# Scan of a state-space layer: all TensorE products of eight heads of a chunk given in one run

## The chip, the core and the metric

The kernel runs on one NeuronCore of a Trainium2 chip. The metric is the device time of one execution in microseconds (us), the lower the better; the time of a kernel is the median of several executions. Engines are named as in the profile: PE (TensorE) multiplies matrices, PEld is its weight load, DVE (VectorE) and ACT (ScalarE) work element by element, POOL (GpSimd) here masks tiles, SP (SyncE) issues most DMAs, and ACT issues some too. Each engine runs its own queue strictly in order and waits at an instruction until the semaphores it needs have been raised by others.

## The reference

One layer of a hybrid backbone is computed twice with the same weights: on a context of 256 tokens and on 2048 latent tokens. Each token row is normalised, multiplied by a wide input matrix, and its columns go to a scan group (Mamba-2 in chunks of 128 tokens, forward and backward) and to a convolution group; both are gated, normalised, and multiplied by an output matrix. What matters here is the scan. For one direction, with chunks of 128 tokens, 16 heads of 64 channels in two groups of eight, and a state of 128 per channel:

```python
    cb = jnp.einsum('bclgn,bcsgn->bgcls', cc, bc)
    y_diag = jnp.einsum('bgcls,bgrcls,bcsgrp->bclgrp', cb, decay_in, xg)
    decay_to_end = jnp.exp(la_cum[..., -1:] - la_cum)
    states = jnp.einsum('bclgn,bgrcl,bclgrp->bcgrpn', bc, decay_to_end, xg)
    ...
    y_off = jnp.einsum('bclgn,bcgrpn,bgrcl->bclgrp', cc, prev, jnp.exp(la_cum))
    y = (y_diag + y_off).reshape(bsz, seqlen, SSD_HEADS, p)
```

`y_diag` are the products inside a chunk, `states` is what a chunk adds to the state, and `y_off` is the part that the state before the chunk gives. `prev` is carried from chunk to chunk.

## The kernel before

The 2304 tokens are 18 tiles of 128 (tiles 0 and 1 are the context). The program has two halves of 10 and 8 tiles. In each half, an `xbc_phase` makes the columns for the scan; then `post` makes the other column blocks, 128 channels at a time, with `gab_unit` (two matrices `gb` and `ga` for the convolution group) and `silu_unit` (`sp`). Each of these blocks is a row of TensorE products of 128x512 or 128x256 in groups of three (high and low parts of both operands, lines 461 to 463). I call these the **dense products**. When both halves are done, a last phase multiplies by the output matrix (`op`).

The forward scan is `pass_a(i)`, one generator for each tile, cut in steps by `yield`. `scan` starts a new tile every seven steps, so that two tiles are in work at once, and `interleave` spreads the steps between the dense products of `post`: tiles 0 to 8 in the first half, 9 to 17 in the second. In the second half `lat_conv` stands there too: rows of very small products (`cp`, line 718), evacuated by DVE (`cvv`, line 722). For tile i and group g (eight heads, in two half-groups hq of four) `pass_a` does:

- `load_lb`: DMAs issued by ACT bring rows of decays, repeated over the partitions, into tiles `lb` (four buffers for each direction). `mask` takes `el` from it on ACT and masks it on POOL, `decay` takes four exponentials on ACT, and `mix` on DVE adds both directions and multiplies by the chunk's `cb`. The finished `lb` is the moving operand of the products inside the chunk, and its buffer is free for the next tile's DMA only when they have read it.
- `weigh(g, d)`: DVE makes `xw`, ACT rounds it to `xwh`, and DVE makes the rest `xwl`. `xwh` and `xwl` have two buffers each: a third `weigh` needs a `state` to have read its two.
- `diag(g, hq)`: four products inside the chunk, 64x128 each, into the PSUM bank `py`; `off(g)`: the part of the state, four products of 128x128 into `po`; `state(g, d)`: three products of 128x512 into `pst`, for direction d.
- `carry`, `keep`, `close`: DVE and ACT empty `po`, `pst` and `py` and store the result.

`diag`, `off` (and `qo`, `cm`, `px`, `pb` elsewhere) work on plain float32, which the profile records as two passes for each product (four products of `py` are x8); `state` and the dense products work on float32r in one pass. Transposes (`px`, half of `pb`) are one pass.

The scan's small PSUM tiles share five banks (`ss`); the dense products have three others (`mm`).

The order of each engine's queue is not the order of the text. The language's scheduler plays the program with a timeline of its own and gives each engine what is ready first; the order in the text is a priority. `InOrder` (lines 67 to 81) overrides this: while `T.on` is true, each TensorE instruction is held behind the TensorE instruction written just before it.

Of the kernel before, what the change touches and what calls it, by code (L numbers as in the profile page):

```python
# [84 lines left out]
def backbone_kernel(ctx, tc, xa, xt_in, cols, rows, wconv, conf_b, gp_row, bg_row, state0, w_mod, w_dt, w_in, w_out,  # L85
# [3 lines left out]
    V, S, T, DMA = (InOrder(tc, e) for e in (nc.vector, nc.scalar, nc.tensor, nc.sync))  # L89
# [5 lines left out]
    def bank(tag, name):  # L95
        return psp.tile([P, 512], F32, tag=tag, name=name, bufs=3 if tag == "mm" else 5)
# [633 lines left out]
    def pass_a(i):  # L730
# [37 lines left out]
        def mix(g, hq):  # L768
            a = E[g, hq, 0]
            V.tensor_tensor(a, a, E[g, hq, 1], ADD)  # L770
            V.tensor_tensor(a, a, cb[:, g, :].unsqueeze(1).to_broadcast([P, 4, P]), MUL)
# [14 lines left out]
        def weigh(g, d):  # L786
            w = pa.tile([P, 512], F32, tag="xw", name=f"xw{i}{g}{d}", bufs=1)
            wh = pa.tile([P, 512], F32R, tag="xwh", name=f"xwh{i}{g}{d}", bufs=2)
            wl = pa.tile([P, 512], F32R, tag="xwl", name=f"xwl{i}{g}{d}", bufs=2)
            c = d * NH + g * 8  # L790
            V.tensor_tensor(b3(w), b3(xt[g]), bh(WS[:, i, c:c + 8]), MUL)
            S.copy(wh, w)
            V.tensor_tensor(wl, w, wh.bitcast(F32), SUB)
            xw[g, d] = wh, wl

        def diag(g, hq):
            if hq == 0:
                py[g] = bank("ss", f"py{i}{g}")
            for t in range(4):
                h = hq * 4 + t  # L800
                j, q = h % 2, h // 2
                T.matmul(py[g][j * HD:(j + 1) * HD, q * P:(q + 1) * P], xt[g][:, h * HD:(h + 1) * HD],  # L802
                         E[g, hq, 0][:, t, :], start=True, stop=True)

        def off(g):
            if i != 0:
                po[g] = bank("ss", f"po{i}{g}")
                for q in range(4):
                    T.matmul(po[g][:, q * P:(q + 1) * P], Sf[g][:, q * P:(q + 1) * P], bc[:, 2 + g, :],  # L809
                             start=True, stop=True)  # L810

        def state(g, d):
            pst[g, d] = bank("ss", f"pst{i}{g}{d}")
            wh, wl = xw[g, d]
            T.matmul(pst[g, d], bth[:, g, :], wh, start=True, stop=False)
            T.matmul(pst[g, d], bth[:, g, :], wl, start=False, stop=False)
            T.matmul(pst[g, d], btl[:, g, :], wh, start=False, stop=True)

        def carry(g):
            if i != 0:  # L820
                V.tensor_tensor(b3(Sf[g]), b3(Sf[g]), bh(eTf[:, i, g * 8:(g + 1) * 8]), MUL)
                w = pa.tile([P, 4, P], F32, tag="yo", name=f"yo{i}{g}", bufs=1)
                V.tensor_tensor(w, po[g].rearrange("p (q l) -> p q l", l=P), el[g], MUL)
                po[g] = w
                V.tensor_tensor(Sf[g], Sf[g], pst[g, 0], ADD)
            else:
                V.tensor_copy(Sf[g], pst[g, 0])

        def keep(g):
            sb = pa.tile([P, 512], F32, tag="sb", name=f"sb{i}{g}", bufs=1)  # L830
            S.copy(sb, pst[g, 1])
            DMA.dma_start(ST[i][:, g * 512:(g + 1) * 512], sb)
# [8 lines left out]
        def close(g):  # L841
            y = yg[g]
            V.tensor_tensor(y, y, py[g].rearrange("p (q l) -> p q l", l=P), ADD)
            if i != 0:
                V.tensor_tensor(y, y, po[g], ADD)
            DMA.dma_start(YP[i][:, g * 512:(g + 1) * 512], y.rearrange("p q l -> p (q l)"))
# [37 lines left out]
        mask(1, 1)  # L884
        skip(1)
        yield
        diag(0, 0)
        off(0)
        state(0, 0)
        weigh(1, 0)  # L890
        mix(1, 0)
        decay(1, 1)
        yield
        diag(0, 1)
        state(0, 1)
        carry(0)
        weigh(1, 1)
        mix(1, 1)
        yield
        diag(1, 0)  # L900
        off(1)
        state(1, 0)
        keep(0)
        close(0)
        yield
        diag(1, 1)
        state(1, 1)
        carry(1)
        yield
        keep(1)  # L910
# [7 lines left out]
    def scan(tiles):  # L918

        gens = [pass_a(i) for i in tiles]  # L920
        live, t = [], 0
        while gens or live:
            if gens and t % 7 == 0:
                live.append(gens.pop(0))
            for g in list(live):
                if next(g, 0) == 0:
                    live.remove(g)
            t += 1
            yield
# [627 lines left out]
```

## Time and profile before

| | us |
|---|---|
| three executions | 1851.51, 1852.80, 1853.14 |
| median | 1852.80 |
| the profiled execution | 1855.05 |
| its span, first to last instruction | 1853.3 |
| first scan (tiles 0 to 8), first to last `py` | 262.5 to about 708 |
| second scan (tiles 9 to 17) | about 918 to 1306 |

The profile is one execution on the core. Busy time is the time in which an engine has an instruction running; products overlap in TensorE, so a TensorE that is busy all the time may still have room. "Idle before" is the time an engine stood still in front of an instruction, followed by what released it. The rows on which the argument rests stand in the prediction.

### The profile page before, as it was taken

Reading aid. Unit: us, or ns where it says so; the run is one execution under the profiler, and the core shown is the slowest. Engines: PE = TensorE matmul, PEld = TensorE weight load, DVE = VectorE, ACT = ScalarE, POOL = GpSimd, SP = SyncE. Lnnn points to the kernel's source line nnn. Section 1 sums busy time; section 2 is a strip of 40 time slices with the busy share of each in tenths; the row PEclk is TensorE's granted clock in tenths of the full one; section 3 lists DMA queues with packets and bytes.
Section 4 is the critical chain, followed back from the end, with each engine's and each line's share of the span. In section 5 each row is a group of like instructions: output and inputs, shape, how many; then the busy total and the mean of one; then the engine's idle time right before and its main releaser. Section 6 shows DMA issues by size and latency. Waiting matters only on the chain.

```text
span 1853.3 us, 29884 instructions
## 1 busy us (share of the span) xinstructions
PE 1793.9 (97%) x11167; PEld 1480.5 (80%) x11167; DVE 1216.5 (66%) x1847; ACT 867.1 (47%) x1960; POOL 172.2 (9%) x281
## 2 busy tenths in 40 slices
PE   5999999999999999999999889999999999999998
PEld 2888887888888888888877667777787888888886
DVE  4597857575666762687457375868347878777763
ACT  4747424444455431744235344554245545454441
POOL 1002001011111000100002011110000101111110
PEclk9999999999999999999999889999999999999999
DMA  9656566554786654545697889694977666656632
GB/s 334 215 198 238 204 212 212 190 201 162 261 267 216 222 182 145 178 170 201 195 207 225 176 239 233 229 236 176 290 223 238 194 184 167 172 171 170 185 103 80
DMA packets 304429, 375.22 MB, mean 202 GB/s; under 512 B 84246, under 2 KB 203670, under 8 KB 304284
## 3 DMA queue, kind: packets, MB, share of 16 engines
q1 hardware_dynamic: 283548, 335.56, 58.1%
q10 hardware_dynamic: 20736, 37.76, 7.3%
q8 instruction: 88, 1.44, 0.3%
q14 instruction: 57, 0.47, 0.1%
HBM read 243.66 MB, written 129.59 MB: 201 GB/s over the span
## 4 chain that ended last, share of the span: by engine, by line
PE 87%; DMA 8%; issue 1%; ACT 1%; DVE 1%; SPq 1%; POOL 0%; ACTq 0%; POOLq 0%; DVEq 0%
PE op L81 21%; PE sp L461 6%; PE sp L462 6%; PE sp L463 6%; PE xp L462 5%; PE xp L461 5%; PE xp L463 5%; PE ga L461 3%; PE ga L463 3%; PE ga L462 3%; PE gb L461 3%; PE gb L463 3%; PE gb L462 3%; DMA lb<-lt 3%; PE py L802 2%; PE po L809 2%
## 5 line engine op out<-in xcount | busy, mean ns | idle before, releaser
L766 ACT ACTIVATE lb<-lb,WB 128x128 f32<-128x128 f32 x576 | 184.5, 391 | 162.7 <-POOL lb L758 156.6
L461 PE MATMUL sp<-hh,wh 128*128 128x512 f32 (+1 forms) x640 | 240.0, 375 | 0.0
L463 PE MATMUL sp<-hh,wl 128*128 128x512 f32 (+1 forms) x640 | 237.1, 371 | 0.0
L462 PE MATMUL sp<-hl,wh 128*128 128x512 f32 (+1 forms) x640 | 237.0, 370 | 0.0
L758 POOL TENSOR_SCALAR_AFFINE_SELECT lb<-lb 128x512 f32<-128x512 f32 x144 | 109.1, 761 | 729.9 <-ACT el L755 400.5
L463 PE MATMUL xp<-hh,wl 128*128 128x512 f32 (+1 forms) x456 | 168.0, 368 | 0.0
L462 PE MATMUL xp<-hl,wh 128*128 128x512 f32 (+1 forms) x456 | 167.8, 368 | 0.0
L461 PE MATMUL xp<-hh,wh 128*128 128x512 f32 (+1 forms) x456 | 167.0, 367 | 0.0
L558 DVE SCALAR_TENSOR_TENSOR cva<-raw,cwh,cva 128x1280 f32<-128x1280 f32 (+1 forms) x96 | 141.9, 1487 | 20.4 <-ACT cva L552 18.2
L463 PEld LDWEIGHTS sp<-hh,wl 128*128 128x128 f32 x640 | 121.3, 189 | 21.1
L461 PEld LDWEIGHTS sp<-hh,wh 128*128 128x128 f32 x640 | 121.6, 190 | 20.7 <-issue 0.2
L462 PEld LDWEIGHTS sp<-hl,wh 128*128 128x128 f32 x640 | 121.6, 190 | 20.0
L461 PE MATMUL ga<-hh,wh 128*128 128x512 f32 (+1 forms) x320 | 121.3, 379 | 6.4 <-DMA wh<-whd 5.5
L75 DVE SCALAR_TENSOR_TENSOR cg<-cg,cv 128x256 f32<-128x256 f32 x240 | 123.0, 512 | 3.3
L461 PE MATMUL gb<-hh,wh 128*128 128x512 f32 (+1 forms) x320 | 120.5, 376 | 0.0
L463 PE MATMUL ga<-hh,wl 128*128 128x512 f32 (+1 forms) x320 | 119.2, 373 | 0.5 <-DMA wl<-wld 0.5
L462 PE MATMUL ga<-hl,wh 128*128 128x512 f32 (+1 forms) x320 | 119.4, 373 | 0.0
L463 PE MATMUL gb<-hh,wl 128*128 128x512 f32 (+1 forms) x320 | 119.0, 372 | 0.0
L462 PE MATMUL gb<-hl,wh 128*128 128x512 f32 (+1 forms) x320 | 118.9, 371 | 0.0
L770 DVE TENSOR_TENSOR lb<-lb,lb 128x512 f32<-128x512 f32 x72 | 50.8, 706 | 90.0 <-ACT lb L766 71.7
L638 DVE SCALAR_TENSOR_TENSOR sth<-sth,sp 128x512 f32<-128x512 f32 (+1 forms) x80 | 50.4, 630 | 75.6 <-ACT sth L637 70.7
L755 ACT ACTIVATE el<-lb 64x256 f32<-64x256 f32 x136 | 56.3, 414 | 88.8 <-DMA lb<-lt 71.2
(273 smaller groups left out, 3832.9 us busy)
## 6 DMA issues: line engine op xcount, KB each, us to landing
lb<-lt ACTq DMA_DIRECT2D x144, 256.0 KB, 4.6
wr<-in_w_in SPq DMA_DIRECT2D x88, 256.0 KB, 4.9
whd<-wh SPq DMA_DIRECT2D x44, 512.0 KB, 3.4
wld<-wl SPq DMA_DIRECT2D x44, 512.0 KB, 5.2
wh<-whd SPq DMA_DIRECT2D x44, 512.0 KB, 5.5
wl<-wld SPq DMA_DIRECT2D x44, 512.0 KB, 5.9
xT<-xb SPq DMA_DIRECT2D x18, 512.0 KB, 4.2
yp<-yg SPq DMA_DIRECT2D x36, 256.0 KB, 4.9
```

The source lines that it names most:

```text
L75: return self._tc.keep_in_program_order(getattr(self._eng, name)(*a, **k))
L81: return lambda *a, **k: self._tc.keep_in_program_order(f(*a, **k))
L461: T.matmul(ps[:, :BN], wh[:, k, :], hh[:, k, :], start=(k == 0), stop=False)
L462: T.matmul(ps[:, :BN], wh[:, k, :], hl[:, k, :], start=False, stop=False)
L463: T.matmul(ps[:, :BN], wl[:, k, :], hh[:, k, :], start=False, stop=(k == KT - 1))
L558: V.scalar_tensor_tensor(a[:, :n], raw[:, t:t + n], cwh[:, ct * 5 + t:ct * 5 + t + 1], a[:, :n], MUL, ADD)
L638: V.scalar_tensor_tensor(th, th, 1.0, ps[:, :BN], ADD, MUL)
L755: S.activation(el[g][rs, q:q + 2, :], E[g, hq, 0][rs, j::2, :], AF.Exp)
L758: G.affine_select(E[g, hq, d], E[g, hq, d], pattern=[[0, 4], [sg, P]], compare_op=ALU.is_ge, fill=NEG, base=0, channel_multiplier=-sg)
L766: S.activation(lb[:, h, :], lb[:, h, :], AF.Exp, bias=WB[:, i, c + h:c + h + 1])
L770: V.tensor_tensor(a, a, E[g, hq, 1], ADD)
L802: T.matmul(py[g][j * HD:(j + 1) * HD, q * P:(q + 1) * P], xt[g][:, h * HD:(h + 1) * HD], E[g, hq, 0][:, t, :], start=True, stop=True)
```

## The change

A new function `burst(g)` gives TensorE, in this order and without anything between, `off(g)`, both `diag(g, hq)` and both `state(g, d)`. It takes the place of the single calls, at the point where the second half of them stood. `weigh(1, 0)` and `weigh(1, 1)`, the weighting of the second group, each stand one step later than before, and `burst(1)` stands directly behind the step that has `weigh(1, 1)`.

```diff
+        def burst(g):
+            T.on = True
+            off(g)
+            diag(g, 0)
+            diag(g, 1)
+            state(g, 0)
+            state(g, 1)
+            T.on = False
+
...
-        diag(0, 0)
-        off(0)
-        state(0, 0)
-        weigh(1, 0)
         mix(1, 0)
         decay(1, 1)
         yield
-        diag(0, 1)
-        state(0, 1)
+        burst(0)
         carry(0)
-        weigh(1, 1)
+        weigh(1, 0)
         mix(1, 1)
         yield
-        diag(1, 0)
-        off(1)
-        state(1, 0)
         keep(0)
         close(0)
-        yield
-        diag(1, 1)
-        state(1, 1)
+        weigh(1, 1)
+        yield
+        burst(1)
         carry(1)
         yield
```

No instruction is added or removed. What the scheduler makes of it is shown at three places of the second half. First TensorE in tile 12, around the first group of heads. A row is the line, the operation, output<-inputs and size, and a count where rows are equal. Before, the two stretches were:

```order
L462 MATMUL ga1_5_3_10179<-hl3_7103,wh3232_1_9646 128x512
L463 MATMUL ga1_5_3_10179<-hh3_7102,wl3232_1_9645 128x512
L802 MATMUL py120_10233<-lb12000_9971,xt120_10068 64x128 x4
L809 MATMUL po120_10238<-bc12_9855,Sf0_259 128x128 x4
L815 MATMUL pst1200_10243<-xwh1200_10134,bth12_10062 128x512
L816 MATMUL pst1200_10243<-xwl1200_10135,bth12_10062 128x512
L817 MATMUL pst1200_10243<-xwh1200_10134,btl12_10063 128x512
L461 MATMUL ga1_5_3_10179<-hh3_7102,wh3232_1_9646 128x512
```

and, 18 dense products further on,

```order
L462 MATMUL gb1_5_4_10268<-hl4_7313,wh4256_1_9642 128x512
L463 MATMUL gb1_5_4_10268<-hh4_7312,wl4256_1_9641 128x512
L802 MATMUL py120_10233<-lb12010_10036,xt120_10068 64x128 x4
L815 MATMUL pst1201_10294<-xwh1201_10184,bth12_10062 128x512
L816 MATMUL pst1201_10294<-xwl1201_10185,bth12_10062 128x512
L817 MATMUL pst1201_10294<-xwh1201_10184,btl12_10063 128x512
L461 MATMUL gb1_5_4_10268<-hh4_7312,wh4256_1_9642 128x512
```

Now, at the place of the second stretch (line 81 is the helper that holds the order):

```order
L462 MATMUL gb1_5_4_10248<-hl4_7313,wh4256_1_9642 128x512
L463 MATMUL gb1_5_4_10248<-hh4_7312,wl4256_1_9641 128x512
L81 MATMUL po120_10270<-bc12_9849,Sf0_259 128x128 x4
L81 MATMUL py120_10275<-lb12000_9957,xt120_10068 64x128 x4
L81 MATMUL py120_10275<-lb12010_10036,xt120_10068 64x128 x4
L81 MATMUL pst1200_10284<-xwh1200_10134,bth12_10062 128x512
L81 MATMUL pst1200_10284<-xwl1200_10135,bth12_10062 128x512
L81 MATMUL pst1200_10284<-xwh1200_10134,btl12_10063 128x512
L81 MATMUL pst1201_10288<-xwh1201_10184,bth12_10062 128x512
L81 MATMUL pst1201_10288<-xwl1201_10185,bth12_10062 128x512
L81 MATMUL pst1201_10288<-xwh1201_10184,btl12_10063 128x512
L461 MATMUL gb1_5_4_10248<-hh4_7312,wh4256_1_9642 128x512
```

The dense row is interrupted once instead of twice, and the state's part comes first. Between this run and that of the second group (`po121`) stand 33 dense products: 9 of `gb1_5_4` and 24 of `ga1_5_4`.

The second place is ACT at the same point of tile 12, from the rounding `xwh1210` to the rounding `xwh1211` of the second group. `el130` and `lb130..` belong to the next tile, 13. Before:

```order
L746 DMA lb13000_10357<-lt1_116 128x512
L792 CAST xwh1210_10248<-xw1210_10247 128x512
L755 ACTIVATE el130_10314<-lb13000_10357 64x256 x2
L766 ACTIVATE lb13000_10357<-lb13000_10357,WB_257 128x128 x4
L746 DMA lb13010_10414<-lt1_116 128x512
L792 CAST xwh1211_10303<-xw1211_10302 128x512
L831 COPY sb120_10351<-pst1201_10294 128x512
```

Now:

```order
L746 DMA lb13000_10343<-lt1_116 128x512
L746 DMA lb13010_10414<-lt1_116 128x512
L792 CAST xwh1210_10297<-xw1210_10296 128x512
L840 COPY sb120_10331<-pst1201_10288 128x512
L755 ACTIVATE el130_10308<-lb13000_10343 64x256 x2
L755 ACTIVATE el130_10308<-lb13010_10414 64x256 x2
L622 ACTIVATE gth1_5_4_10322<-gb1_5_4_10248 128x512
L766 ACTIVATE lb13000_10343<-lb13000_10343,WB_257 128x128 x4
L766 ACTIVATE lb13010_10414<-lb13010_10414,WB_257 128x128 x4
L792 CAST xwh1211_10338<-xw1211_10337 128x512
```

Both DMAs of the next tile's `lb` now stand together, and the second rounding stands behind two `el`, a `gth` and both sets of exponentials, where it stood behind one `el` and one set.

The third place is TensorE in tile 11, first group, beside a row of the small products `cp2` of `lat_conv` (`cp2_0` and `cp2_1`, two `ss` banks, 64 products in turn). Before, the row followed the first stretch of the group:

```order
L802 MATMUL py110_9724<-lb11000_9313,xt110_9485 64x128 x4
L809 MATMUL po110_9729<-bc11_9260,Sf0_259 128x128 x4
L815 MATMUL pst1100_9734<-xwh1100_9605,bth11_9479 128x512
L816 MATMUL pst1100_9734<-xwl1100_9606,bth11_9479 128x512
L817 MATMUL pst1100_9734<-xwh1100_9605,btl11_9480 128x512
...
L718 MATMUL cp2_0_9761<-cx2_9345,kt2_9703 32x64
L718 MATMUL cp2_1_9762<-cx2_9345,kt2_9703 32x64
```

Now it stands ahead of the whole run, with six dense products between:

```order
L718 MATMUL cp2_1_9742<-cx2_9331,kt2_9703 32x64
L461 MATMUL ga1_4_3_9720<-hh3_7102,wh3104_1_9177 128x512
L462 MATMUL ga1_4_3_9720<-hl3_7103,wh3104_1_9177 128x512
L463 MATMUL ga1_4_3_9720<-hh3_7102,wl3104_1_9176 128x512
L461 MATMUL ga1_4_3_9720<-hh3_7102,wh3104_1_9177 128x512
L462 MATMUL ga1_4_3_9720<-hl3_7103,wh3104_1_9177 128x512
L463 MATMUL ga1_4_3_9720<-hh3_7102,wl3104_1_9176 128x512
L81 MATMUL po110_9813<-bc11_9254,Sf0_259 128x128 x4
L81 MATMUL py110_9818<-lb11000_9299,xt110_9485 64x128 x4
L81 MATMUL py110_9818<-lb11010_9390,xt110_9485 64x128 x4
```

The six `pst` products follow as in tile 12. Six dense products between a `cp` row and a run of a group stand also in tiles 9 (first group), 13 and 15 (second group), and twelve in tile 15 (first group).

## The prediction

> **What bounds the kernel now.** I began with the page's first and fourth parts, busy time and the chain that ended last.
>
> ```profile
> span 1853.3 us, 29884 instructions
> PE 1793.9 (97%) x11167; PEld 1480.5 (80%) x11167; DVE 1216.5 (66%) x1847; ACT 867.1 (47%) x1960; POOL 172.2 (9%) x281
> PE 87%; DMA 8%; issue 1%; ACT 1%; DVE 1%; SPq 1%; POOL 0%; ACTq 0%; POOLq 0%; DVEq 0%
> ```
>
> PE is busy 97% of the span and makes up 87% of the chain. So a change pays only if it shortens PE's own row, and costs only if it makes PE wait. The two scans differ, though, and the average hides it. The windows below are the first scan's part, the second scan, and the last phase; the columns are length, then busy time of PE, PEld, DVE, ACT and POOL, the granted clock, the DMA share and GB/s.
>
> ```profile
> 200.00:830.00 630.00, 629.10 (x3455) 527.24 (x3454) 409.48 (x645) 294.19 (x668) 56.41 (x95) 1.00 0.60 201
> 930.00:1310.00 380.00, 353.61 (x3707) 278.83 (x3706) 251.51 (x430) 173.20 (x428) 45.69 (x64) 0.95 0.80 213
> 1310.00:1853.00 543.00, 532.46 (x2570) 446.17 (x2569) 363.07 (x534) 248.78 (x597) 46.69 (x54) 1.00 0.62 182
> ```
>
> In the first scan PE stands still for 0.9 us of 630: time saved on PE is time saved. In the second it stands still for 26.4 us of 380, the clock is at 0.95, and the DMA engines are at 0.80: there PE is often the one that waits. For whom, the list of PE's waits says (total, times, longest):
>
> ```profile
> PE ga L461 <- DMA wh<-whd: 5.5, 1, 5.5
> PE px L778 <- issue: 5.3, 2, 4.1
> PE cp L718 <- DVE cvv L722: 4.4, 1, 4.4
> PE pst L815 <- DVE cvv L722: 3.5, 1, 3.5
> PE pst L815 <- ACT xwh L792: 1.7, 1, 1.7
> ```
>
> These are single long waits in the second scan, behind transfers and behind DVE and ACT work that itself waited.
>
> **What the change saves on PE.** Tile 6, first group, in the timeline (start, duration, line, tiles, count): two stretches, each from the last dense product before it to the first one behind it.
>
> ```profile
> 579.43 0.39 PE L463 MATMUL sp<-hh,wl 128*128 128x512 f32 x1
> 579.75 0.66 PE L802 MATMUL py<-lb,xt 128*64 128x128 f32 x8
> 580.33 1.16 PE L809 MATMUL po<-bc,Sf 128*128 128x128 f32 x8
> 581.25 0.47 PE L815 MATMUL pst<-xwh,bth 128*128 128x512 f32 x1
> 581.56 0.39 PE L816 MATMUL pst<-xwl,bth 128*128 128x512 f32 x1
> 581.79 0.40 PE L817 MATMUL pst<-xwh,btl 128*128 128x512 f32 x1
> 582.02 0.40 PE L461 MATMUL sp<-hh,wh 128*128 128x512 f32 x1
> ...
> 585.91 0.39 PE L463 MATMUL sp<-hh,wl 128*128 128x512 f32 x1
> 586.23 0.66 PE L802 MATMUL py<-lb,xt 128*64 128x128 f32 x8
> 586.81 0.50 PE L815 MATMUL pst<-xwh,bth 128*128 128x512 f32 x1
> 587.15 0.40 PE L816 MATMUL pst<-xwl,bth 128*128 128x512 f32 x1
> 587.39 0.40 PE L817 MATMUL pst<-xwh,btl 128*128 128x512 f32 x1
> 587.63 0.28 PE L461 MATMUL sp<-hh,wh 128*128 128x256 f32 x1
> ```
>
> Starts count here, since products overlap. Products of 512 columns follow each other by 0.23 us (581.56 to 581.79). Going from dense to `py` takes 0.32, from `py` to the first `pst` and on to the second 0.58 to the start and then 0.34. So a stretch pays for changing from one kind to the other, about 0.09 going in and 0.11 and more coming out. The stretches are 2.59 and 1.72 us, together **4.31**.
>
> The burst is not in the trace; I put it together. Dense to `po`: full-width float32 behind float32r, shown by `cm` in the last phase:
>
> ```profile
> 1470.51 0.62 PE L81 MATMUL op<-woh,pl 128*128 128x512 f32 x2
> 1470.97 0.38 PE L81 MATMUL cm<-v,ones 128*128 128x128 f32 x2
> 1471.11 0.71 PE L81 MATMUL op<-woh,ph 128*128 128x512 f32 x2
> ```
>
> Two dense products and the step to `cm` take 0.46, so going in costs the ordinary 0.23. Four `po` take 0.92 (580.33 to 581.25). `po` to `py` has no row: I add the 0.09 that `py` costs behind dense work, with bounds 0 and 0.19 (twice that, rounded). Eight `py`: 0.58 for four with their way out, and four more at the pace of a pass of `po`, 0.92/8 = 0.115, so 1.04; bounds 0.87 (the further four at half the price) and 1.16 (twice 0.58). Six `pst`: 0.82 for three with their way out (586.81 to 587.63) and three at 0.23, so 1.51. Sum 0.23 + 1.01 + 1.04 + 1.51 = 3.79, and 0.23 for the dense step that now lies elsewhere: 4.02. **A group saves 0.29 us**, bounds 0.07 and 0.55. There are 36 groups (tile 0 has no `po`; its two `py` stretches come to about the same), so 10.4 us in all, bounds 2.5 and 19.8: 5.2 in each scan.
>
> The Trainium skill speaks against this term: "TensorE: Matmul & The Clock Gate", section "Step-by-step: what each phase is for", says that TensorE pulls the next weight load ahead of running products, so that next weights load beside current work. By that alone a change of kind would be free and this term nothing; the rows (0.32 against 0.23) disagree, and the row decides.
>
> The first scan's 5.2 I count in full: PE had no idle time there, and DVE (409 of 630) and ACT (294) have room. Of the second's I count **half, 2.6**: where a transfer or DVE is what PE waits for, an earlier PE only waits longer. Bounds 0 and 5.2.
>
> **What it adds: a wait at the second burst.** Products that moved later meet inputs that are ready; the exception is `weigh(1, d)`. Its buffers `xwh` are free only after both `state(0, d)`, now at the end of the first burst, and ACT's queue has the next tile's `el` and exponentials ahead of `xwh` of (1, 1). Those need a DMA into `lb` buffers that `diag` of the first burst frees. So PE's first burst releases a DMA, ACT waits for it, and behind ACT stands PE's second burst, with all dense products behind that. Tile 12 in the trace (ACT, ACTq its DMA issues; then DVE, then the landing time over all `lb` transfers, least, median, most):
>
> ```profile
> 1082.48 0.33 ACTq L746 DMA_DIRECT2D lb<-lt  x1
> 1083.61 0.61 ACT L792 CAST xwh<-xw 128x512 fp32r<-128x512 f32 x1
> 1088.41 0.85 ACT L755 ACTIVATE el<-lb 64x256 f32<-64x256 f32 x2 [4.19 <-DMA lb<-lt]
> ...
> 1094.14 0.60 ACT L622 ACTIVATE gth<-gb 128x512 f32<-128x512 f32 x1
> 1095.10 1.28 ACT L766 ACTIVATE lb<-lb,WB 128x128 f32<-128x128 f32 x4 [0.35 <-POOL lb L758]
> ```
> ```profile
> 1092.97 0.68 DVE L793 TENSOR_TENSOR xwl<-xw,xwh 128x512 fp32r<-128x512 f32 x1
> ```
> ```profile
> DMA to landing us min/median/max: 3.0/4.6/7.9
> ```
>
> From the freed `lb` to a finished `xwl`: issue 0.33, landing 4.6, two `el` 1.70, `gth` 0.60, mask 0.35, two sets of exponentials 2.56, `xwh` 0.61, `xwl` 0.68, together 11.4; with the 5.9 that this transfer took (1082.48 to 1088.41) 12.7. From the same point PE has: six `pst` 1.51, 33 dense 7.6, into and through `po` and `py` 2.28, three `pst` 0.82, together 12.2. So it is even: nothing at the median landing, 0.5 at 5.9, 2.5 at 7.9. Tiles 12 and 16 have this order; 10 and 14 leave out one or both sets of exponentials, and the others have nothing of `lb` there, or, in the first scan, at least 9.8 us of dense work (18 products of 512 columns and 48 of 256, in tile 2) between the bursts. I take **1 us each for tiles 12 and 16: 2 us**; bounds 0 and 5.
>
> **And a wait for banks.** A stretch before held three of the five `ss` banks, so a pair of `cp` banks could still be waiting for DVE; a burst needs four. Where a `cp` row stands just ahead, the last bank of the burst must be one that `cvv` has emptied. Rows of PE and of DVE, in tile 11 and in tile 13:
>
> ```profile
> 1023.02 1.48 PE L718 MATMUL cp<-cx,kt 32*32 32x64 f32 x128
> 1139.41 1.48 PE L718 MATMUL cp<-cx,kt 32*32 32x64 f32 x128
> ```
> ```profile
> 1034.89 1.29 DVE L722 SCALAR_TENSOR_TENSOR cvv<-cp,cbb 128x512 f32<-128x512 f32 x2 [2.22 <-DMA kd<-in_wconv]
> ...
> 1143.20 1.28 DVE L722 SCALAR_TENSOR_TENSOR cvv<-cp,cbb 128x512 f32<-128x512 f32 x2
> ```
>
> DVE had emptied them 11.7 and 3.6 us after the row's end. PE has six dense products, `po`, `py` and three `pst` until then: 1.4 + 2.28 + 0.82 = 4.5. At 3.6 nothing waits. At 11.7 the burst of tile 11 waits 7.2; but the same lateness stopped PE before as well, at the next `cp` row (4.4) and at tile 11's last `pst` (3.5), and those two then shrink. I set old against new: **0**, bounds -4 (both old waits gone, the new one halved) and 10 (the five places named, 2 us each).
>
> The moved `px` (behind some eight dense products, where it stood directly behind `pb`) can cover part of its 5.3 us of waits; I leave that in the half above.
>
> **Sum.** -5.2 - 2.6 + 2.0 + 0 = -5.8 us. On the profiled execution (1855.05, span 1853.3) this gives 1849.2; that run lies 2.25 above the median of the three shown. On the median of 1852.8 it gives **1847.0 us**.
>
> **The rivals.**
> All of it arrives: no wait at the bursts, and the second scan keeps its 5.2, so 1852.8 - 10.4 = 1842.4. For it: PE's waits in the second scan are few long events, and between them it was full. Against: DMA at 0.80.
> The second scan gives all back: -5.2 + 2.0 gives 1849.6. For it: 26.4 us of idle there, none of PE's own doing.
> The saving isn't there, because `po` to `py` and the longer run cost what the second change of kind did: 0.07 a group, -2.5 + 2.0 gives 1852.3. This is also where the Trainium skill's rule above would lead. Against it: both ways into `py` above cost the same 0.32.
> Slower: the banks decide. If DVE is late at the five `cp` places by 2 us more than PE has room, PE waits 10 us, and an idle PE also loses clock, as the windows around tile 11's 3.5 us wait show:
>
> ```profile
> 1047.70:1051.10 3.40, 0.32 (x6) 0.08 (x2) 1.33 (x3) 2.35 (x8) 0.64 (x1) 1.00 0.01 3
> 1051.10:1054.50 3.40, 2.98 (x11) 2.59 (x12) 3.36 (x7) 2.02 (x1) 0.40 (x1) 0.50 0.29 88
> ```
>
> 3.4 us at half the clock lose 1.7 us; two such add 3.4. Together -5.8 + 10 + 3.4 = +7.6, so 1860.4. It comes out slower than before once the five waits pass 1.2 us each, a `cvv` that is done 5.7 us after its row. For it: 11.7 in one of the two rows. Against: 3.6 in the other. The Trainium skill, "TensorE: Matmul & The Clock Gate" (section "HAM oscillation — how this bites in real kernels"), sets the bound at idle gaps over about 3.4 us; by it waits of 2 us would lose no clock, and this rival would end at 1857.0.
>
> **How the numbers follow.** Forecast 0.40, all arrives 0.20, second scan gives back 0.20, no saving 0.07, slower 0.13. The range 1839.5 to 1857 takes in the first four, the lower end for a change of kind dearer than I took (a few us of the way to 0.55 a group), and the near half of the slower case (1852.8 to 1857). A measurement here tells 0.2% (3.7 us) from no change, so the limits are 1849.1 and 1856.5: faster 0.60 (most of the forecast, all of the first rival, a quarter of the second), same 0.27, slower 0.13.
>
> **What would show it.** A burst in the new timeline should take about 3.8 us from dense to dense where nothing waits, `po` first at 0.23. PE's busy time in the first scan should shrink with the span and its idle time stay near 0.9 us. In the second scan waits of `pst` for `xwl` or `xwh` should appear at tiles 12 and 16, with `lb` landings behind them on ACT, and one for a bank at tile 11, behind `cvv`. The prediction is wrong in size if a burst takes 4.2 or more, and wrong in kind if PE's idle time in the first scan grows by several us, or if the waits of the second sum to over 35 us.

## The result, and the profile after

| | before | after |
|---|---|---|
| median of 12 executions, us | 1854.9 | 1845.4 |
| ratio of the times, with its 95% interval | | 0.9946 (0.9931 to 0.9962) |
| profiled execution (span), us | 1855.05 (1853.3) | 1848.29 (1846.6) |

The change made the kernel faster by 0.54%, about 10 us: on the median of 1852.8 this is 1842.8 (1840.0 to 1845.8). Forecast were 1847.0, with 1839.5 to 1857.0. The sign and the range hold, but the time came from other places than the forecast said. One of the twelve executions before took 6255 us; it counts in the median and not in the ratio. The first and fourth parts of the page after:

```profile
span 1846.6 us, 29922 instructions
PE 1784.9 (97%) x11167; PEld 1489.9 (81%) x11167; DVE 1212.8 (66%) x1847; ACT 866.2 (47%) x1960; POOL 170.6 (9%) x281
PE 77%; DMA 10%; ACT 4%; DVE 4%; issue 3%; SPq 1%; POOL 0%; ACTq 0%; DVEq 0%; POOLq 0%
```

The 38 instructions more are none of those counted for the five engines. PE lost 9.0 us of busy time (1793.9 to 1784.9) and its share of the chain fell from 87 to 77%: more of the chain now runs through DMAs, ACT and DVE. PE's longest waits in the two scans (total, times, longest; `issue` is time in which PE waited for nothing that the profile shows):

```profile
PE sp L461 <- DVE sth L638: 7.6, 2, 4.9
PE pst L81 <- DVE cvv L722: 7.5, 2, 6.8
PE pst L81 <- ACT xwh L792: 4.9, 1, 4.9
PE cp L718 <- issue: 3.5, 2, 2.6
PE px L778 <- issue: 3.1, 2, 2.1
```

The last four are the second scan's, where 5.5 (`ga` for `wh`), 5.3 (`px`), 4.4 (`cp`) and 3.5 (`pst` for `cvv`) had led. The first is new, and in the first scan.

To see where time went I cut both runs at the same four dense products. Windows before (length, then busy time of PE, PEld, DVE, ACT, POOL, the granted clock, DMA share, GB/s), the first and the second scan:

```profile
256.79:741.45 484.66, 483.76 (x2729) 403.55 (x2728) 302.54 (x517) 217.65 (x535) 50.42 (x80) 1.00 0.62 206
925.08:1315.27 390.19, 363.80 (x3752) 287.25 (x3750) 254.69 (x435) 174.42 (x430) 45.69 (x64) 0.95 0.81 214
```

and after:

```profile
258.06:746.88 488.82, 481.15 (x2729) 409.47 (x2728) 301.64 (x517) 216.33 (x535) 50.35 (x80) 0.99 0.61 205
930.53:1308.30 377.77, 355.35 (x3751) 289.76 (x3750) 252.27 (x436) 174.93 (x430) 44.19 (x64) 0.96 0.84 221
```

Each pair holds the same products. The first scan became **4.2 us longer**: PE's idle time (length less busy) grew from 0.9 to 7.7. The second became **12.4 us shorter**: idle fell from 26.4 to 22.4, busy time by 8.5. The forecast was -5.2 and -0.6. Busy time also holds what half clock costs, which I take as half of the time that PE was busy at half clock: 0 and 15.3 us in the two scans before, 4.3 and 13.0 after. Without it **TensorE's own work fell by 6.9 us in the first scan and 6.1 in the second**.

**The saving.** The burst of tile 2's first group in the timeline (start, duration, line, tiles, count):

```profile
375.94 0.39 PE L463 MATMUL ga<-hh,wl 128*128 128x512 f32 x1
376.17 1.05 PE L81 MATMUL po<-bc,Sf 128*128 128x128 f32 x8
377.15 1.09 PE L81 MATMUL py<-lb,xt 128*64 128x128 f32 x16
378.17 0.50 PE L81 MATMUL pst<-xwh,bth 128*128 128x512 f32 x1
...
379.44 0.40 PE L81 MATMUL pst<-xwh,btl 128*128 128x512 f32 x1
379.67 0.28 PE L461 MATMUL gb<-hh,wh 128*128 128x256 f32 x1
```

It takes 379.67 - 375.94 = 3.73 us, in steps of 0.23, 0.98, 1.02 and 1.50, where 3.79 was put together. With the dense step 3.96, against 4.31 in two stretches: **0.35 a group**, 12.6 us for 36.

**The wait that wasn't foreseen.** ACT in tile 5 after: the square of an input row of the second half (`xin`), line 337, stands ahead of `sth`, which empties the dense bank:

```profile
536.21 1.06 ACT L337 ACTIVATE xin<-xin 128x1024 f32<-128x1024 f32 x1 [6.08 <-DMA xin<-in_xa]
...
537.78 0.57 ACT L840 COPY sb<-pst 128x512 f32<-128x512 f32 x1
543.28 1.06 ACT L337 ACTIVATE xin<-xin 128x1024 f32<-128x1024 f32 x1 [4.92 <-DMA xin<-in_xa]
...
544.33 0.58 ACT L637 ACTIVATE sth<-sp 128x512 f32<-128x512 f32 x1
```

and PE, which waits for that bank:

```profile
545.68 0.80 PE L461 MATMUL sp<-hh,wh 128*128 128x512 f32 x1 [4.86 <-DVE sth L638]
```

Before, the same `sth` stood between two such squares, and the second of them waited 1.5 us only:

```profile
542.22 0.57 ACT L637 ACTIVATE sth<-sp 128x512 f32<-128x512 f32 x1
544.32 1.06 ACT L337 ACTIVATE xin<-xin 128x1024 f32<-128x1024 f32 x1 [1.52 <-DMA xin<-in_xa]
```

No line of the change touches these squares, but the new order has two squares more ahead of that `sth`. SP issued the DMAs of these two at 530.43 and 537.39, the second only when the square of 536.21 had ended, so squares in a row cost a landing each. That the scheduler moved them because the products left other gaps on ACT is my reading; no run shows it.

**The two waits that were.** PE and DVE in tile 11's first burst, with the bank that `cvv` must empty:

```profile
1027.89 0.40 PE L81 MATMUL pst<-xwh,btl 128*128 128x512 f32 x1
1035.05 0.79 PE L81 MATMUL pst<-xwh,bth 128*128 128x512 f32 x1 [6.76 <-DVE cvv L722]
```
```profile
1034.30 1.29 DVE L722 SCALAR_TENSOR_TENSOR cvv<-cp,cbb 128x512 f32<-128x512 f32 x2 [11.26 <-DMA cv<-cvv]
```

7.2 was forecast here, 6.8 it is. Tile 12's second burst: ACT, then PE.

```profile
1081.20 0.40 ACT L766 ACTIVATE lb<-lb,WB 128x128 f32<-128x128 f32 x1 [3.61 <-POOL lb L758]
1081.27 0.33 ACTq L746 DMA_DIRECT2D lb<-lt  x1
...
1085.55 1.71 ACT L755 ACTIVATE el<-lb 64x256 f32<-64x256 f32 x4 [2.08 <-DMA lb<-lt]
1087.29 0.60 ACT L622 ACTIVATE gth<-gb 128x512 f32<-128x512 f32 x1
1087.90 2.44 ACT L766 ACTIVATE lb<-lb,WB 128x128 f32<-128x128 f32 x8
...
1090.25 0.60 ACT L792 CAST xwh<-xw 128x512 fp32r<-128x512 f32 x1
```
```profile
1090.90 0.79 PE L81 MATMUL pst<-xwh,bth 128*128 128x512 f32 x1 [4.89 <-ACT xwh L792]
```

This is the chain that was written down, link by link; its length is off (below).

### The profile page after: what moved, and what is told of

It reads as the page before. It is cut to its first block, busy times and chain, and to the rows that moved or that the text cites. A ratio compares the mean times of both kernels' runs of the same rounds, so it can differ in the third digit from the quotient of the medians.

```text
span 1846.6 us, 29922 instructions
## 1 busy us (share of the span) xinstructions
PE 1784.9 (97%) x11167; PEld 1489.9 (81%) x11167; DVE 1212.8 (66%) x1847; ACT 866.2 (47%) x1960; POOL 170.6 (9%) x281
## 4 chain that ended last, share of the span: by engine, by line
PE 77%; DMA 10%; ACT 4%; DVE 4%; issue 3%; SPq 1%; POOL 0%; ACTq 0%; DVEq 0%; POOLq 0%
PE op L81 21%; PE sp L461 6%; PE sp L463 5%; PE sp L462 5%; PE xp L461 4%; PE xp L462 4%; PE xp L463 4%; DMA lb<-lt 4%; PE gb L463 3%; PE gb L461 3%; PE gb L462 3%; PE ga L461 3%; PE ga L462 3%; PE ga L463 3%; PE pst L81 2%
## 5 line engine op out<-in xcount | busy, mean ns | idle before, releaser
L461 PEld LDWEIGHTS xp<-hh,wh 128*128 128x128 f32 x456 | 86.0, 189 | 14.8 <-ACT raw L546 0.5
L462 PEld LDWEIGHTS xp<-hl,wh 128*128 128x128 f32 x456 | 86.0, 189 | 14.1
```

The lines of the kernel that those rows point to most:

```text
L461: T.matmul(ps[:, :BN], wh[:, k, :], hh[:, k, :], start=(k == 0), stop=False)
L462: T.matmul(ps[:, :BN], wh[:, k, :], hl[:, k, :], start=False, stop=False)
```

## The experiments

Twelve runs, in three rounds. Ratios are to the kernel before, timed on the same chip. Diffs are against the changed kernel unless said otherwise.

| kernel | ratio (95% interval) | first scan, us | idle | second scan, us | idle |
|---|---|---|---|---|---|
| before | | 484.7 | 0.9 | 390.2 | 26.4 |
| changed | 0.9946 (0.9931 to 0.9962) | 488.8 | 7.7 | 377.8 | 22.4 |
| again | 0.9923 (0.9901 to 0.9945) | 488.5 | 7.4 | 376.1 | 24.0 |
| cvv2 | 0.9936 (0.9915 to 0.9956) | 486.6 | 6.9 | 375.9 | 22.1 |
| sq17 | 0.9932 (0.9911 to 0.9954) | 485.8 | 6.6 | 371.0 | 18.0 |
| wx13 | 0.9920 (0.9896 to 0.9943) | 487.8 | 7.2 | 372.1 | 21.2 |
| first | 0.9988 (0.9972 to 1.0005) | 486.8 | 6.9 | 385.7 | 23.3 |
| second | 0.9941 (0.9920 to 0.9963) | 484.4 | 0.4 | 382.7 | 28.4 |
| kinds | 0.9990 (0.9971 to 1.0009) | 483.5 | 5.2 | 384.7 | 30.4 |
| pyfirst | 0.9915 (0.9886 to 0.9944) | 490.0 | 8.8 | 378.3 | 26.3 |
| xlate14 | 0.9886 (0.9867 to 0.9905) | 476.6 | 0.1 | 374.5 | 22.0 |
| allfix | 0.9903 (0.9887 to 0.9919) | 480.9 | 2.3 | 375.0 | 21.4 |
| before_rows | 1.0067 (1.0044 to 1.0091) | 491.3 | 5.3 | 403.2 | 36.3 |
| after_rows | 0.9963 (0.9945 to 0.9981) | 486.7 | 7.5 | 374.4 | 20.8 |

The scans are lengths between the same dense products as above, from one profiled execution each, idle is length less PE's busy time. The profiled execution lies within 5 us of the kernel's median, except for `again` (6 above), `after_rows` (7 below), `before_rows` (11 above) and `pyfirst` (15 above), whose lengths are to be read with that. Two executions with the same order on PE, DVE, ACT and POOL differ too: the second scan took 377.8 and 376.1 us (changed, `again`).

### The three waits, one at a time

**again**: the changed kernel once more.

> The changed kernel itself, once more. Theory A (the change's own size is fixed by the order of the queues): 0.993 to 0.997 of the kernel before, a burst of 3.73 us from dense to dense where nothing waits, and the same three long waits of PE again: the last state product of tile 11's first burst behind DVE's cvv (6.8 us), the last state of tile 12's second burst behind ACT's xwh (4.9), and sp behind DVE's sth near 541 us (4.9). Theory B (the waits are accidents of one execution): at least one of the three is missing or under half as long.

Theory A holds for the waits: 6.0 us at tile 11, 5.7 at tile 12, 3.7 near 541 us. The ratio lies just below its 0.993. The waits belong to the order, not to one execution.

**cvv2**: a second buffer.

```diff
-        vt = lp.tile([P, 32, 64], F32, tag="cvv", name=f"cvv{j}", bufs=1)
+        vt = lp.tile([P, 32, 64], F32, tag="cvv", name=f"cvv{j}", bufs=2)
```

> The changed kernel with two buffers for cvv instead of one, so that DVE need not wait until the store of the row before has read the single one; the order on every engine is that of the changed kernel. Theory A (the bank wait at tile 11 is a real cost, 6.8 us of standing and some 1.5 to 2.5 us at half clock behind it): 6 to 9 us faster than the changed kernel run beside it, and the wait of pst for cvv at tile 11 is gone. Theory B (the late store is only a sign of busy DMA queues, and the row after it waits as long for another transfer): 0 to 2 us faster, with a wait of about the same length at the next cp or kd.

Theory B holds, with 0.9936 against 0.9923 for the unedited kernel beside it. The first burst of tile 11 runs through, and its second one, which had not waited, waits for `cvv` in its place. This time `cvv` is late because DVE stands 8.0 us ahead of it at a `yg`, for the DMA that stores an earlier one:

```profile
1045.34 0.77 PE L81 MATMUL pst<-xwh,bth 128*128 128x512 f32 x1 [6.31 <-DVE cvv L722]
```

**sq17**: one pair of rows swapped on ACT, by an order edge from `sth` of that block to the square of xin17.

```diff
-                    with tc.issue_after(anchor[0].ins):
+                    with tc.issue_after((anchor17 if i == 17 else anchor)[0].ins):
                         S.activation(xt, xt, AF.Square, accum_out=ms)
```

> The changed kernel with two neighbouring rows of ACT's queue swapped: the square of the input row xin17 goes behind the evacuation sth of the dense block before it, as it stood before the change. Theory A (the change cost 4.9 us there, because ACT waits for the DMA of xin17 ahead of the sth that frees the dense bank, and about 2.4 us more at half clock): 5 to 7.5 us faster than the changed kernel run beside it, no gap of PE near 541 us. Theory B (sth and PE then wait for something else in the same convoy, such as lb or the store behind SP): 0 to 3 us faster, with a wait of PE for another releaser between 540 and 575 us.

Theory B again, in its wait; the time (0.9932) is not better. The gap at 541 us is gone, and 20 us on PE waits longer than it did there (2.8 us in the changed kernel):

```profile
PE sp L461 <- DVE sth L640: 5.2, 1, 5.2
PE px L780 <- issue: 1.4, 1, 1.4
```

The square still stops ACT for 3.9 us; now other work stands behind it.

**wx13**: on ACT, `el` of tile 13's first half-group goes behind the last `xwh` of tile 12, by an order edge in `mask`.

```diff
+                    late = tc.issue_after(last_wh[0].ins) if i == 13 and (g, hq) == (0, 0) else nullcontext()
+                    with late:
-                    S.activation(el[g][rs, q:q + 2, :], E[g, hq, 0][rs, j::2, :], AF.Exp)
+                        S.activation(el[g][rs, q:q + 2, :], E[g, hq, 0][rs, j::2, :], AF.Exp)
```

> The changed kernel with the exponentials el of tile 13 (first half-group) held on ACT behind the rounding xwh of tile 12's last weighting. Theory A (tile 12's second burst waits because ACT has the next tile's el, a gth and both sets of exponentials ahead of xwh(1,1), as forecast): the wait of 4.9 us falls to about 1.5 (DVE's own xw is done 3.4 us before ACT rounded it), and the kernel is 3 to 6 us faster than the changed kernel beside it, half clock counted. Theory B (the chain through DVE, whose queue is full of cg rows there, is the later one): the wait falls by under 1 us and the time stays within 2 us.

The wait fell to what theory A says, 0.57 + 0.77 = 1.3 us, so the chain is the one described. But the gain did not come: 0.9920 against 0.9923 for the unedited kernel beside it. In tile 13's second burst, one tile later, 0.8 us of waiting for `cvv` became

```profile
1134.58 0.77 PE L81 MATMUL pst<-xwh,bth 128*128 128x512 f32 x1 [4.47 <-DVE cvv L722]
```

### Which half, and which products

**first** and **second**: the new tail of `pass_a` under `if i < 9:` or `if i >= 9:`, the old one for the other tiles.

> The run of eight heads (and the later weightings) in tiles 0 to 8 alone; tiles 9 to 17 as in the kernel before. Theory A (from the profiles: in the first scan TensorE's own work falls by 6.9 us, but ACT's queue, released in bursts, makes dense blocks wait some 7 us near 541 and 567 us, and half clock behind them costs 4): 0 to 5 us slower than the kernel before, with PE's two waits of sp for sth in the first scan and the waits of the second scan as before the change. Theory B (the forecast: the first scan keeps its saving whole): 5 to 7 us faster.

> The run of eight heads in tiles 9 to 17 alone; tiles 0 to 8 as in the kernel before. Theory A (the gain sits in the second scan: 6.0 us less work of TensorE, some 4 less waiting, 2 to 6 less at half clock): 10 to 15 us faster than the kernel before, faster than the changed kernel beside it by 0 to 5 us, and no wait of PE between 260 and 720 us beyond 1 us. Theory B (the forecast: the second scan keeps half its saving and gets new waits): 0 to 2 us faster.

`second` alone gives all of the changed kernel's gain (0.9941), as theory A says, and `first` alone gives none that is clear (0.9988; theory A, 0 to 5 us slower, was too dark). In its profile the first scan is 2.1 us longer than before and has PE's waits of 4.7 and 2.1 us at 541 and 568. The forecast's -5.2 for the first scan lies at the interval's end. But the ratio is not the first scan's alone: in `first`'s second scan PE has the order of before, while some 40 rows each of DVE and ACT stand elsewhere, and it took 385.7 us instead of 390.2. The changed kernel was not timed beside `second`; against its 0.9946 and 0.9923 of other rounds `second` is no faster.

**kinds**: the state products stand apart again.

```diff
             diag(g, 1)
-            state(g, 0)
-            state(g, 1)
...
+        state(0, 0)
+        weigh(1, 0)
         mix(1, 0)
         decay(1, 1)
         yield
         burst(0)
+        state(0, 1)
         carry(0)
-        weigh(1, 0)
+        weigh(1, 1)
         mix(1, 1)
         yield
+        state(1, 0)
         keep(0)
         close(0)
-        weigh(1, 1)
         yield
         burst(1)
+        state(1, 1)
         carry(1)
```

> The run holds only off and both diag; the state products stand apart again, state(0) a step ahead of the run and state(1) behind it, and weigh(1, d) where it stood before the change. Theory A (what costs is a change between the dense products' kind and plain float32 narrow products; a state product is a dense product in kind and costs nothing more when it stands alone): TensorE's own work in both scans within 1.5 us of the changed kernel's, pst alone between dense products at 0.23 us each, the wait of pst for xwh at tile 12 gone; the time equal to the changed kernel's or up to 5 us less. Theory B (each interruption of the dense row costs, whatever its kind): 36 more interruptions at 0.1 to 0.3 us, TensorE's own work 4 to 10 us more than in the changed kernel.

On the cost of a change of kind theory A holds. A state product between dense ones:

```profile
369.12 0.39 PE L463 MATMUL gb<-hh,wl 128*128 128x512 f32 x1
369.34 0.39 PE L815 MATMUL pst<-xwh,bth 128*128 128x512 f32 x1
369.57 0.39 PE L816 MATMUL pst<-xwl,bth 128*128 128x512 f32 x1
369.80 0.39 PE L817 MATMUL pst<-xwh,btl 128*128 128x512 f32 x1
370.02 0.39 PE L461 MATMUL gb<-hh,wh 128*128 128x512 f32 x1
```

Every step is 0.22 or 0.23: it costs nothing to stand alone. What is paid for is going into and out of the narrow plain float32 products, and joining both `diag` with `off` saves all there is: with one state behind it such a run takes 3.03 us, and three state products at 0.23 elsewhere make 3.72, against 3.73. But the gain is gone (0.9990). PE's idle time in the second scan is 30.4 us against 22.4 in the changed kernel, where I had expected one wait less. `pst` of (g, 0) now holds its bank from a step ahead of the run until `carry`, which may be the reason: `pst` waits for `cvv` four times, 12.2 us in all, where it did twice, 7.5. That was not tested. Against the changed kernel's this profile is 5.9 us longer: 6.9 more in the second scan, 5.3 less in the first, and 3.6 more in the last phase, behind both scans, for which I have no cause.

**pyfirst**: both `diag` ahead of `off` in the run.

> The run with both diag ahead of off. Theory A (going from dense products into py costs 0.32 and into po the ordinary 0.23, as the rows have it): a run of 3.75 to 3.85 us instead of 3.73, so 1 to 4 us more in all. Theory B (what was saved is only the number of changes): a run of 3.73 or less, and the time of the changed kernel.

Theory B holds, within 0.01: going in costs 0.32 instead of 0.23, but `po` then takes 0.91 for 0.98 and `pst` 1.48 for 1.50. The run of tile 2 takes 3.74 us, and the time is that of the changed kernel in other rounds (0.9915).

### What holds ACT, and what paces the second scan

**xlate14**: the squares of xin14 to xin17 wait for a `sth` of the first scan's last third.

```diff
             c = S.activation(th, ps[:, :BN], AF.Tanh, scale=0.5)
+            if (half, c0, j, b) == (0, GS0, 0, 2):
+                late.append(c)
...
-                    with tc.issue_after(anchor[0].ins):
+                    with tc.issue_after((late if i >= 14 else anchor)[0].ins):
                         S.activation(xt, xt, AF.Square, accum_out=ms)
```

> The changed kernel with the squares of the input rows xin14 to xin17 held on ACT behind a sth of the first scan's last third (about 630 us), away from the place where PE waits for sth at 541 and 567 us; TensorE's order is that of the changed kernel. Theory A (ACT stands still twice for the DMAs of xin16 and xin17, 11 us in all, and everything of lb and sth queues behind it): no wait of PE over 1 us between 530 and 580 us, the first scan falls from 488.8 to 476 to 480 us, the kernel is 6 to 11 us faster than the changed one (ratio to the kernel before 0.987 to 0.990). Theory B (the runs free the lb buffers late and in pairs, and that alone makes ACT late): a wait of sp for sth of 2.5 us or more stays near 565 us, and the kernel gains 0 to 4 us.

Theory A holds in all its numbers, and this is the fastest kernel here: **0.9886**, 1831.9 us against 1852.3. Windows of both scans:

```profile
258.43:735.02 476.59, 476.49 (x2730) 406.67 (x2728) 299.80 (x517) 216.35 (x535) 49.89 (x80) 1.00 0.61 210
918.66:1293.20 374.54, 352.57 (x3751) 287.47 (x3750) 254.06 (x439) 175.14 (x432) 44.10 (x64) 0.97 0.84 224
```

The first scan has no idle time and full clock, as before the change, so its 476.5 against 483.8 us is TensorE's own work: 7.3 us less, 0.40 for each of the 18 groups. The burst above gives 0.35, so 6.3; the other 1.0 us I have not placed. What the squares had done shows in ACT's waits, after and then before (530 to 570 and 530 to 565 us):

```profile
ACT xin L337 <- DMA xin<-in_xa: 11.0, 2, 6.1
ACT lb L766 <- POOL lb L758: 6.3, 1, 6.3
```
```profile
ACT lb L766 <- POOL lb L758: 6.1, 4, 2.8
ACT xin L337 <- DMA xin<-in_xa: 5.9, 3, 2.6
```

Two waits of 6.1 and 4.9 us in the place of three of at most 2.6.

**allfix**: xlate14, cvv2 and wx13 together.

> The squares held as in the kernel before this one, cvv with two buffers, and el of tile 13 behind xwh of tile 12: all three named waits of the changed kernel attacked at once. Theory A (the waits add up): PE's idle time in the second scan falls from 22 to 12 us or less, and the kernel is 5 to 10 us faster than with the squares alone. Theory B (the second scan is paced by its transfers, and a wait taken away at one place returns at the next): 18 us or more of idle time there, and the time of the kernel with the squares alone within 3 us.

Theory B holds: 21.4 us idle in the second scan and no gain on top of xlate14. The waits taken away come back at other places.

**before_rows**, **after_rows**: the same edit on the kernel before and on the changed one.

```diff
-            DMA.dma_start(x[rs], GL[j][:, 256:].rearrange("(g a) (r w) -> a r g w", a=4, w=64)[a])
+            DMA.dma_start(x[rs], GL[j][rs, 256:].rearrange("g (r w) -> g r w", w=64))
...
-            DMA.dma_start(CV[c0:c0 + 32, 256:].rearrange("c (r w) -> r c w", w=64), vt[u * 32:(u + 1) * 32])
+            DMA.dma_start(CV[c0:c0 + 32, 256:].rearrange("c (r w) -> c r w", w=64), vt[u * 32:(u + 1) * 32])
```

> The kernel before with the loads cx and the stores cv of the convolution rows moved as whole rows of 8 KB instead of pieces of 256 bytes: the same bytes, instructions and buffers, but the rows land permuted, so the convolution group is computed from permuted data. Theory A (the waits of the second scan, 26.4 us, and 15.3 us lost at half clock come from DMA engines jammed by small pieces): PE's idle time in the second scan below 12 us, clock loss below 7, and 18 to 30 us faster than the kernel before. Theory B (it is the bytes, or the order of the queues): less than 6 us faster, idle time above 20.

> The changed kernel with the same loads and stores as whole rows, the convolution group again from permuted data. Theory A (with the jam gone, the change is worth TensorE's own work alone: 6.9 and 6.0 us, less some 11 us in the first scan through ACT's queue, which this edit doesn't touch): 0 to 5 us faster than the kernel before with whole rows. Theory B (what the change gained in the second scan beyond the 6.0 us is its own doing and not the jam's): 8 to 12 us faster than that kernel, as without the edit.

My theory A falls. The DMA share in the second scan fell from 0.81 to 0.70 (before_rows) and from 0.84 to 0.73 (after_rows), and PE's idle time did not follow: 36.3 and 20.8 us. So with the small pieces gone the waits were not. The edit also gave DVE and ACT another order in both kernels, so the runs do not clear the pieces of every part. With that order the change was worth more than either theory says, 1863.9 to 1846.7. What sets the 18 to 36 us of idle time in the second scan stays open; the runs show that it changes when the queues' order does, and that removing one wait, or three, doesn't remove it.

## Why the prediction was right, and where it was wrong

- **The saving a group** (0.29, bounds 0.07 to 0.55) was the right mechanism, 0.06 too small: 0.35. Of the 0.09 put on `po` to `py` 0.06 is there: four `po` and the step to `py` take 0.98, forecast 0.92 + 0.09; `py` took 0.02 less and `pst` 0.01 less than forecast. That four more products of `py` cost 0.46, though they are eight passes, was taken without a row, and came out. The Trainium skill's rule that was weighed against it ("TensorE: Matmul & The Clock Gate", section "Step-by-step: what each phase is for", next weights load beside running products) would have made this nothing; xlate14's 7.3 us at full clock decide against that.
- **The first scan in full, -5.2**: this step failed. Its work did shrink, by more (7.3). But "PE had no idle time there, and DVE and ACT have room" took a share of busy time for room in a queue. ACT was busy 45% of the first scan (217.65 of 484.66), and still a square that waits for its DMA, ahead of `sth` in the order, stopped PE. The forecast's own test said it: wrong in kind if PE's idle time in the first scan grows by several us. It grew by 6.8, and half clock behind the gaps cost 4.7 more (481.15 busy against 476.49 in xlate14). With the four squares held and TensorE's order the same, xlate14 has neither, so in that scan it was the squares.
- **Half of the second scan's saving, -2.6**: failed on the other side. Nearly all of it came: TensorE's own work fell by 6.1 there (0.35 x 18 = 6.3), and by 3.7 to 7.1 in the other kernels that have the run in that scan, since between its waits PE was full; the rival "all of it arrives" had said so. With 4.0 less idle time and 2.3 less lost at half clock this makes the 12.4. Old waits went: 5.5 for `wh`, whose DMA SP issued at 1057.30 where it had been 1062.58 (landing 7.8 us later), and 2.2 of `px`'s 5.3, probably through the dense products now ahead of it, which the forecast mentioned without a number. How much of this is the change's own and how much the luck of an order, the runs don't settle.
- **The wait at the second burst**, 1 us each at tiles 12 and 16: right in its chain, in tile 12 off in size, 4.9, and absent in tile 16. The chain was started at the moment when PE's first burst frees `lb` (about 1074 us); ACT issued that DMA at 1081.27, because it stood until 1076.31, and 3.6 us more until 1081.20, before exponentials whose masks were late. From the issue to the rounding it then took 9.6 us, less than the 10.7 that the forecast's links give without the `xwl` of 0.68. A chain through a queue starts where the engine gets to the row.
- **The banks**, 0: right, place and size. 6.8 at tile 11 for 7.2 forecast, and the old waits of 4.4 and 3.5 went. With 0.8 of `pst` at tile 13 and 0.8 of `gb`, which are new, PE waits 8.3 us for `cvv` against 7.9.
- **The sum.** The first scan came out 9.4 us above its forecast and the second 11.8 below. That the total lies 4 us from 1847.0 is the sum of two errors, not a hit.

## What to carry to other kernels

Count a saving on the bounding engine in full, also in a stage that waits often (here 6.1 us of 6.3 came), but look in the new order for what now stands ahead of each instruction that empties its banks: an operation that waits for a DMA there costs a whole landing, however idle its engine is on average. Here four such operations were tied behind a later instruction, where they waited for nothing; that was worth 0.4 to 0.6%, where the change alone gave 0.5 to 0.8%. In a stage with many long waits don't pay for one of them: taken away singly, they came back within a group or two, and three at once gained nothing either.

## What the runs showed of the hardware

Half clock follows gaps of PE that are much shorter than I had expected, and comes in whole pieces. In the changed kernel PE stands still for 2.76 us between dense products of the first scan (PE, then the window behind it; the clock is the third number from the end):

```profile
570.08 0.50 PE L461 MATMUL sp<-hh,wh 128*128 128x512 f32 x1 [2.76 <-DVE sth L638]
```
```profile
571.40:574.80 3.40, 3.40 (x10) 2.63 (x9) 3.40 (x6) 1.71 (x5) 0.64 (x1) 0.50 1.05 398
```

In xlate14 a gap of 1.24 us was enough:

```profile
937.25 0.73 PE L461 MATMUL gb<-hh,wh 128*128 128x512 f32 x1 [1.24 <-DVE gth L625]
937.77 0.63 PE L462 MATMUL gb<-hl,wh 128*128 128x512 f32 x1
938.20 0.63 PE L463 MATMUL gb<-hh,wl 128*128 128x512 f32 x1
```
```profile
937.30:940.70 3.40, 3.40 (x13) 2.89 (x15) 0.13 (x1) 0.00 (x0) 0.00 (x0) 0.50 0.85 297
940.70:944.10 3.40, 3.40 (x27) 2.81 (x26) 3.28 (x6) 1.21 (x2) 0.00 (x0) 1.00 1.10 258
```

PE was busy for all of the 3.4 us at 0.50, and dense products followed each other by 0.43 us instead of 0.23. But the gap was not alone: in the 3.41 us ahead of that piece the small products `cp` took another 1.24 us. And in the same run a gap of 2.14 us, from 1164.65 to 1166.79, left the clock at 1.00 on both sides.

The clock's records in the fourteen traces tell the cases apart. Between 200 and 1340 us the pieces at half clock in one trace begin a whole number of 3.413 us apart, and each lasts one, two, three or five times that. So the scan can be cut into such windows. After a window at full clock without `cp`, half clock came 62 times, each time with 1.56 us or more of idle time in the window (all but one with 1.90 or more), and full clock stayed 4119 times, with 1.92 or less. With `cp` in the window, 0.96 us of idle time was the least that brought half clock, and 1.63 the most that didn't. The gap of 2.14 us fell into two windows, 1.35 and 0.80.

The Trainium skill ("TensorE: Matmul & The Clock Gate", section "HAM oscillation — how this bites in real kernels") sets the bound at gaps over about 3.4 us; the runs here disagree. About 1.9 us inside one window was enough, less beside `cp`, and a piece of 3.4 us in which PE is busy throughout costs 1.7 us (half of 3.40).
